# A hybrid attention and recurrence layer on one core: fewer and larger slot transfers, evictions on two engines, attention work written later

## The chip, the cores and the metric

The kernel runs on one core of a Trainium2 chip. The core has a matrix engine (TensorE, PE in the profile; its weight loads stand apart as PEld), a vector engine (VectorE, DVE), a scalar engine (ScalarE, ACT), a general engine (GpSimd, POOL) and an engine that here only issues transfers (SyncE, SP). Each takes its own instructions in the order in which they were written into its stream, and waits on semaphores for the others. Transfers between main memory and the on-chip memory run on 16 DMA engines; nearly all are issued by SP, one after the other.

The metric is the device time of one execution, in microseconds (us). A profile is one execution; it gives the time of every instruction, and the clock that was granted to TensorE.

## The reference

One layer, for 256 prompt tokens (context) and 1024 latent tokens: a normalisation, one large input projection, and two groups of heads side by side, whose outputs go through one output projection.

```
h = rmsnorm(x, norm_g) * (1 + scale) + shift
u = h @ w_in
q, k, v, g_a, u_b, g_b = split(u)
o_a = diff_attention(q, k_all, v_all, lam, ...) * silu(g_a)      # 8 heads, two score maps each
o_b, s_final = rwkv_branch(u_b, g_b, s0, lp)                     # 16 heads of 64
x = x + gate * (concat([o_a, o_b]) @ w_out)
y = rmsnorm(x, final_g)
```

Attention subtracts one softmax from another before it multiplies the values. The recurrent branch runs once forward and once backward over the tokens, with a 64 x 64 state per head:

```
def diff_attention: p = softmax(q @ k / 8);  a = p[0] - lam * p[1];  o = a @ v
def step(S, inp):
    sa = einsum('bhvk,bhk->bhv', S, -kk_t)
    S = S * w_t + sa[..., None] * b_t + v_t[..., None] * k_t
    return S, einsum('bhvk,bhk->bhv', S, r_t)
```

Beside the two outputs the layer returns the new keys and values of the prompt and the final states.

## The kernel before

**First stage.** The input projection, in blocks of 128 columns, with the shifts, decays and rotations that follow from each block. What the recurrence needs later goes to main memory: `kt` (keys, corrections and the small triangular matrices of a chunk), `ra` (queries), `vb` (values), and a triangular inverse (`td`) that GpSimd works out (`inverse`).

**Second stage** (`mix_phase`). The recurrence runs over chunks of 32 tokens. Two chunks make a part, eight chunks (a segment of 256 tokens) an item; there are 10 items, 40 parts and 80 chunks, called ticks here. Four pairs of heads run at a time, as two duos (`w` = 0 and 1), each with both directions. Each duo has two slots, used in turn by even and odd parts. A slot is a tile `L` (the matrices of a part) and a tile `R` (its right-hand sides: state, values, corrections).

- `load_part` (L766) loads a part into its slot, one part ahead: after a slot's last reader, the output products of the part before the last. `load_inv` (L787) loads the inverses into a tile `Tb`, one per duo, from three buffers (`TBUF`).
- `prep` (L794) multiplies the inverses into the slot: 32 small products into the bank `yb` (L802) and four copies by ScalarE into `L` (L805). It is written ahead of the second tick of the part before.
- `step` is one tick: correction products (L894), four copies of them per duo into `R` by ScalarE (L899); state products (L908), a multiplication by the decays into the next state by VectorE (L917); output products (L931) and one copy per duo into `ys` (L933). `store_y` writes four ticks of outputs.
- `fill` is called at two places of a tick. It lets attention run on by as many pieces as a credit allows (`RATE`, 0.86 of an even spread), and moves the inverse, the normalisations (`norm`) and the output projections (`project`) on by a piece.

Attention takes 80 blocks (8 heads, 10 blocks of 128 queries). A block over latent tokens has three chunks of keys per score map: scores (L1047), scaling with running minimum by VectorE (L1050), exponential by ScalarE (L1058); then the weight of the second map (L1070 to L1072), the combination of the two maps (`combine`, L1078), transposes (`trans`, L1086, copied by ScalarE at L1088) and the products with the values (L1101). Before the change the combination, transposes and values of a block are written among the scores of the block after it.

`norm` turns the recurrence's outputs into gated ones, `output` does so for attention, with `NDEL` and `ODEL` pauses. `project(j)` multiplies two heads of each group by their rows of `w_out` (L1286 to L1288) and adds to a sum in main memory (`acc`: loaded at L1268, added at L1280, stored at L1282); the last one, `final`, adds the residual and normalises. Projections 0 and 1 are started when the first five items are done, 2 and 3 after the last item.

The order on each engine is made by a scheduler that simulates the program; the order of the text is the priority, and `ahead(500)` raises the priority of what stands under it.

## Time and profile before

| | |
|---|---|
| median of 3 runs | 2642.7 us (2634.27 to 2647.06) |
| the profiled execution | 2639.98 us, of which 2637.7 us from the first to the last instruction (the span) |
| first stage, and the way into the second | 0 to 1243 us |
| recurrence (80 ticks) with attention, normalisations, projections 0 and 1 | 1243 to 2395 us |
| rest: last attention blocks, projections 2 and 3, final normalisation | 2395 to 2638 us |
| busy over the span: PE, DVE, ACT, POOL | 90%, 56%, 48%, 45% |
| mean clock granted to TensorE | 0.939 |

Times in profile rows are in us from the start of the span, unless marked ns. In a row of waits stand the waiting engine, tile and line, what ended the wait, then the total, the number and the longest. In a row of a group stand line, engine, operation, tiles (out<-in), shapes and count, then busy time and mean ns of one, then the engine's idle time ahead of them and what ended it.

### The profile page before, as it was taken

The page shows a single profiled execution, that of the slowest core. Times are in us where ns is not written, and L with a number is a line of the kernel's source. Part 1 is how long each engine was busy: PE and PEld are TensorE (multiplying, and loading weights), DVE is VectorE, ACT ScalarE, POOL GpSimd, SP SyncE. Part 2 cuts the span into 40 slices and gives each one's busy share as a digit, 9 for nine tenths or more (in the row PEclk, how much of TensorE's full clock was granted, in tenths as well). Part 3 has the DMA queues.
Part 4 walks back from the last instruction along what each step waited for, and adds up shares of the span by engine and source line. Part 5 has one row for each costly group of instructions (what it writes and reads, how often), then busy time and mean ns, then how long its engine had stood idle before and what let it go on. Part 6 is the DMA issues. An engine that isn't in the chain of part 4 may idle for free. (4 is left out here: it accounts for less than half of the span.)

```text
span 2637.7 us, 61554 instructions
## 1 busy us (share of the span) xinstructions
PE 2361.2 (90%) x23907; PEld 1908.8 (72%) x23907; DVE 1475.6 (56%) x2960; ACT 1274.8 (48%) x2928; POOL 1199.6 (45%) x1735
## 2 busy tenths in 40 slices
PE   6999999999999999998688888888889898898886
PEld 4788888888888888786466766666666676676664
DVE  5656565555455655434457556664455455566466
ACT  3334443333333433322476666766556357674243
POOL 4234344243433443375365525747467542125386
PEclk9999999999999999998798889889989999999997
DMA  7465656565645565567878777878867887676534
GB/s 237 111 165 131 177 147 176 135 169 161 160 129 155 136 176 131 167 158 185 176 155 187 162 160 145 184 164 191 211 155 194 203 198 171 141 171 220 176 104 161
DMA packets 532418, 437.63 MB, mean 166 GB/s; under 512 B 161991, under 2 KB 466291, under 8 KB 532128
## 3 DMA queue, kind: packets, MB, share of 16 engines
q1 hardware_dynamic: 530032, 427.96, 64.9%
q0 software_dynamic: 2096, 5.75, 1.1%
q8 instruction: 188, 3.08, 0.5%
q14 instruction: 102, 0.84, 0.1%
HBM read 258.69 MB, written 163.86 MB: 160 GB/s over the span
## 5 line engine op out<-in xcount | busy, mean ns | idle before, releaser
L1047 PE MATMUL sc<-ka,q 128*128 128x512 f32 (+1 forms) x832 | 296.7, 457 | 20.2 <-DVE pb L1050 12.3
L1050 DVE TENSOR_SCALAR_CACHE_REDUCE pb<-sc,mn 128x512 f32<-128x512 f32 x256 | 191.7, 749 | 135.1 <-PE sc L1047 110.4
L1101 PE MATMUL po<-vk,aT 128*128 128x128 f32 x1600 | 244.8, 296 | 9.1 <-ACT aT L1088 8.6
L1058 ACT ACTIVATE pb<-pb,mn 128x1536 f32<-128x1536 f32 (+1 forms) x160 | 218.4, 1366 | 60.2 <-DVE pb L1050 58.7
L1101 PEld LDWEIGHTS po<-vk,aT 128*128 128x128 f32 x1600 | 221.3, 205 | 29.4 <-ACT aT L1088 12.2
L479 POOL TENSOR_SCALAR ta<-ta,ka 128x256 f32<-128x256 f32 x80 | 88.1, 1101 | 297.8 <-DVE bk L477 297.7
L734 POOL TENSOR_TENSOR tmp<-aw,tt 128x31 f32<-128x31 f32 (+15 forms) x310 | 164.6, 531 | 127.9 <-DMA aw<-kt 54.9
L456 ACT COPY km<-ptk 64x256 f32<-64x256 f32 x320 | 117.4, 367 | 192.1 <-PE ptk L453 165.7
L899 ACT COPY R<-bank 32x128 f32<-32x128 f32 x640 | 163.4, 255 | 68.7 <-PE bank L894 59.4
L917 DVE TENSOR_TENSOR R<-bank,wc 64x256 f32<-64x256 f32 x312 | 131.4, 421 | 113.5 <-PE bank L908 98.4
L736 POOL TENSOR_TENSOR tt<-tt,tmp 128x31 f32<-128x31 f32 (+15 forms) x310 | 182.4, 588 | 18.2
L1047 PEld LDWEIGHTS sc<-ka,q 128*128 128x128 f32 x832 | 145.6, 208 | 55.7 <-DVE pb L1050 21.5
L1078 DVE SCALAR_TENSOR_TENSOR pb<-pb,cc,pb 128x512 f32<-128x512 f32 (+1 forms) x208 | 170.6, 866 | 2.5
L805 ACT COPY L<-yb 32x384 f32<-32x384 f32 x312 | 146.3, 469 | 40.1 <-PE yb L802 35.9
L802 PE MATMUL yb<-L,Tb 32*32 32x96 f32 x2496 | 96.1, 261 | 76.3 <-DMA L<-kt 68.7
L450 DVE TENSOR_TENSOR km<-pg,msk 128x512 f32<-128x512 f32 x80 | 55.1, 689 | 183.5 <-PE pg L449 168.7
L1050 DVE TENSOR_SCALAR_CACHE_REDUCE pb<-sc 128x512 f32<-128x512 f32 (+1 forms) x160 | 101.2, 635 | 91.2 <-PE sc L1047 75.3
L1088 ACT COPY aT<-pa 128x512 f32<-128x512 f32 (+1 forms) x208 | 115.9, 570 | 62.9 <-PE pa L1086 60.5
L1086 PE MATMUL pa<-ident,pb 128*128 128x128 f32 x800 | 133.2, 292 | 14.0 <-ACT acc L1278 7.8
L802 PEld LDWEIGHTS yb<-L,Tb 32*32 32x32 f32 x2496 | 62.6, 111 | 105.9 <-DMA L<-kt 56.3
L908 PEld LDWEIGHTS bank<-R,L 128*64 128x64 f32 x2560 | 99.3, 151 | 54.6 <-ACT R L899 23.7
L908 PE MATMUL bank<-R,L 128*64 128x64 f32 x2560 | 122.9, 243 | 16.7 <-ACT R L899 16.4
(355 smaller groups left out, 6463.2 us busy)
## 6 DMA issues: line engine op xcount, KB each, us to landing
kt<-km SPq DMA_DIRECT2D x160, 256.0 KB
L<-kt SPq DMA_DIRECT2D x80, 512.0 KB
acc<-acc SPq DMA_DIRECT2D x50, 512.0 KB
ra<-ra SPq DMA_DIRECT2D x160, 128.0 KB
L<-ra SPq DMA_DIRECT2D x160, 128.0 KB
R<-vb SPq DMA_DIRECT2D x320, 32.0 KB
y<-ys SPq DMA_DIRECT2D x160, 64.0 KB
yn<-y SPq DMA_DIRECT2D x20, 512.0 KB
```

The lines of the kernel that those rows point to most:

```text
L734: e.tensor_tensor(mv, aw[:n, t, t + 1:CH].unsqueeze(2).broadcast_to([n, w, j]), tt[:n, t:t + 1, 0:j].broadcast_to([n, w, j]), op=ALU.mult)
L736: e.tensor_tensor(tt[:n, t + 1:CH, 0:j], tt[:n, t + 1:CH, 0:j], mv, op=ALU.add)
L802: nc.tensor.matmul(pp[32 * q:32 * q + 32, n:n + 96], Tb[96:128, e, HN * q + c, :], L[96:128, e, q // 2, q % 2, c, 0:96], start=True, stop= ...
L805: nc.scalar.copy(L[96:128, :, q // 2, q % 2, :, 0:96], pp[32 * q:32 * q + 32, 0:192 * HN].rearrange("p (e c y) -> p e c y", e=2, y=96))
L899: nc.scalar.copy(R[96:128, k, e, :, hv(h)], bank[w][u:u + 32, 0:128].rearrange("p (d v) -> p d v", d=2))
L908: nc.tensor.matmul(bank[w][hv(h), o_:o_ + 64], L[:, e, h, d, k, 0:64], R[:, k, e, d, hv(h)], start=True, stop=True, tile_position=(0, 64 * h))
L1047: nc.tensor.matmul(sc, q[:, v, m, qc], ka[:, m, 0:kn], start=(v == 0), stop=(v == 1))
L1050: nc.vector.tensor_scalar(pm[:, c * 512:c * 512 + kn], sc, -0.125, mn[:, c - 1:c] if c else None, op0=ALU.mult, op1=ALU.min, accum_out=mn[ ...
L1058: nc.scalar.activation(v, v, AF.Exp, bias=mn[:, c:c + 1], scale=-1.0, accum_out=B["l3"][:, m, k:k + 1])
L1078: nc.vector.scalar_tensor_tensor(a, B["p"][1][:, v], B["cc"], a, op0=ALU.mult, op1=ALU.add)
L1086: nc.tensor.transpose(pt[:, t * P:(t + 1) * P], B["p"][0][:, 512 * c + t * P:512 * c + (t + 1) * P], ident)
L1101: nc.tensor.matmul(po, B["aT"][c][:, t * P:(t + 1) * P], vk[:, t, :], start=(c == 0 and t == 0), stop=(c == last and t == nt - 1))
```

## The change

- The scratch tensors `ra`, `kt` and `y` are laid out by duo (for `y` by four pairs), so that a duo's `kt` and `ra` are each one transfer, and a duo's values of two chunks one per direction (`R` is turned to [chunk, direction, pair] for it). A part takes 2 transfers of `kt`, 4 of `vb`, 2 of `ra`, and 1 of the inverses for both duos: 9 where there were 16. Outputs are stored in 4 transfers per four ticks instead of 8. `norm` reads its input in 2 transfers instead of 1.
- `Tb` is one tile for both duos, in one buffer instead of three tiles of half the size.
- The first duo's `prep` is written behind the correction copies of a part's second tick, the second duo's behind the tick's output products. Both stood ahead of that tick.
- The correction copies of the second duo go to VectorE. Only evictions are raised in priority now, the products are not. The output products stand beside the state products: the second `fill` comes after both.
- Attention: weight and combination are written at the end of the block itself, transposes among the next block's second scores, the values behind them or in the block after that; the sum of the exponentials goes straight to its place without a copy, and there is a third buffer for the transposed weights.
- Pace: 1.06 of an even spread in the first half of the ticks and 0.68 in the second, instead of 0.86 throughout; longer pauses in `norm`, `output` and the projections; projections 2 and 3 are started after the seventh item instead of the last.
- In `final` the residual is added by VectorE instead of GpSimd.

```diff
-RATE = 0.86
-TBUF = 3
-NDEL = 6
-ODEL = 8
+RATES = (1.06, 0.68)
+TBUF = 1
+NDEL = 10
+ODEL = 14
...
-    scratch("ra", [H, 5, NF, HD, 2, 2, HN * HD])
-    scratch("kt", [H, 5, NF, HD, 2, 2, HN * P])
+    scratch("ra", [H // 2, 5, NF, HD, 2, 2, 2, HN * HD])
+    scratch("kt", [H // 2, 5, NF, HD, 2, 2, 2, HN * P])
...
     def load_part(j):
...
-            nc.sync.dma_start(L[64:128].rearrange("r e h d c y -> r e (h d c y)"),
-                              s["kt"][p:p + 2, sg + 1, f].rearrange("e r h d y -> r e (h d y)"))
-            for e in range(2):
-                nc.sync.dma_start(L[0:64, e, :, :, :, 64:128].rearrange("r h d c y -> r (h d c) y"),
-                                  s["ra"][p + e, sg + 1, f].rearrange("r h d (c y) -> r (h d c) y", y=HD))
+            nc.sync.dma_start(L[64:128].rearrange("r e h d c y -> r (e h d c y)"),
+                              s["kt"][p // 2, sg + 1, f].rearrange("r e h d y -> r (e h d y)"))
+        load_inv(j)
+        for w in duos:
...
             for d in range(2):
                 t0 = tok0(sg, d) + CH * HN * (NF - 1 - f if d else f)
-                for c in range(HN):
-                    t1 = t0 + CH * (HN - 1 - c if d else c)
-                    nc.sync.dma_start(R[64:96, c, :, d, :], s["vb"][t1:t1 + CH, p * P:(p + 2) * P].rearrange("t (e v) -> t e v", e=2))
+                src = s["vb"][t0:t0 + CH * HN, p * P:(p + 2) * P].rearrange("(c t) y -> t c y", t=CH)
+                nc.sync.dma_start(R[64:96, :, d].rearrange("t c e v -> t c (e v)"), src[:, ::-1] if d else src)
+            nc.sync.dma_start(L[0:64, :, :, :, :, 64:128].rearrange("r e h d c y -> r (e h d c) y"),
+                              s["ra"][p // 2, sg + 1, f].rearrange("r e h d (c y) -> r (e h d c) y", y=HD))
...
     def load_inv(j):
-        for w in duos:
-            Tb = cp.tile([P, 2, 4 * HN, CH], F32, tag="Tb", name=f"Tb{w}_{j}", bufs=TBUF)
...
+        Tb = cp.tile([P, NL, 4 * HN, CH], F32, tag="Tb", name=f"Tb{j}", bufs=TBUF)
...
     def step(j, k, fill):
-        with ahead(HPC):
-            for w in duos:
...
-                        nc.scalar.copy(R[96:128, k, e, :, hv(h)], bank[w][u:u + 32, 0:128].rearrange("p (d v) -> p d v", d=2))
-        fill(0)
         with ahead(HPC):
             for w in duos:
...
+                        (nc.vector.tensor_copy if w else nc.scalar.copy)(
+                            R[96:128, k, :, e, hv(h)], bank[w][u:u + 32, 0:128].rearrange("p (d v) -> p d v", d=2))
+        later_prep = k == HN - 1 and j + 1 < n_part
+        if later_prep:
+            prep(j + 1, 0, yb)
+        fill(0)
...
-        fill(1)
...
+        for w in duos:
+            nc.scalar.copy(ysb[m, g][:, c % 4, 2 * w:2 * w + 2], bank[w][:, P:2 * P].rearrange("p (e v) -> p e v", e=2))
+        if later_prep:
+            prep(j + 1, 1, yb)
+        fill(1)
...
-        q.dma_start(y.rearrange("p t d v -> p t (d v)"), s["y"][p // 2, cols].rearrange("(t p) d v -> p t (d v)", p=P))
+        for t in range(2):
+            q.dma_start(y[:, t].rearrange("p d (h v) -> p (d h) v", h=2),
+                        s["y"][p // NL, g0 * P + t * P:g0 * P + (t + 1) * P, :, :, p % NL // 2].rearrange("p d h v -> p (d h) v"))
...
-            if p is not None:
-                weight(p)
-                combine(p, 0)
-            if pp is not None:
-                values(pp, len(st[pp]["ch"]) - 1)
+                if c < nk - 1 and vp:
+                    old_values()
+                    yield 0.87
+            while vp:
+                old_values()
                 yield 0.87
...
+            for c in range(max(nk, kp_)):
+                if c < kp_:
+                    trans(p, c)
+                    yield 0.43
+                if c < nk:
+                    scores(n, 1, c)
+                    yield cost
+            if new:
+                weight(n)
+                for c in range(nk):
+                    combine(n, c)
+            if kp_ > 1:
+                values(p, 0)
+                yield 0.87
...
-                nc.gpsimd.tensor_tensor(x, x, y, op=ALU.add)
+                nc.vector.tensor_tensor(x, x, y, op=ALU.add)
...
-            state["credit"] += rate / 2
+            state["credit"] += total / (4 * n_tick) * RATES[2 * state["t"] // n_tick]
...
-        if k == HN - 1 and j + 1 < n_part:
-            for w in duos:
-                prep(j + 1, w, yb)
...
-        if sg == 3:
+        if sg == (3 if m < 5 else 0):
```

What this does to the order on the engines is shown at three places. In the rows the tiles `L_11593` and `L_11583` are the second duo's slots (odd and even parts), `L_11573` and `L_11563` the first duo's; `bank_12298` and `bank_12299` (before) and `bank_12282` and `bank_12283` (now) are the banks of the first and the second duo.

TensorE before, ahead of the second duo's `prep` for part 15: from the last reading of the second duo's odd slot by output products to the first `prep` products on the newly loaded slot.

```order
L931 MATMUL bank_12299<-R_11594,L_11593 32x64 x8
L931 MATMUL bank_12298<-R_11564,L_11563 32x64 x8
L1047 MATMUL sc_6_1_2_17587<-ka_2_15907,q_1_15910 128x512 x2
L1047 MATMUL sc_7_0_0_17700<-ka_0_14697,q_1_15910 128x512 x2
L1101 MATMUL po_5_17599<-vk_0_14700,aT_5_0_17555 128x128 x4
L1086 MATMUL pa_5_2_17604<-ident,pb_12302 128x128 x4
L1101 MATMUL po_5_17599<-vk_1_16177,aT_5_1_17597 128x128 x4
L1047 MATMUL sc_7_0_1_17704<-ka_1_15904,q_1_15910 128x512 x2
L894 MATMUL bank_12299<-R_11584,L_11583 32x64 x8
L802 MATMUL yb<-L_11593,Tb_15_17192 32x96 x16
```

TensorE now, two parts later (part 17): the last rows ahead of the same duo's `prep`, with its first. The last reading of the slot `L_11593` stands four rows further up.

```order
L893 MATMUL bank_12283<-R_11584,L_11583 32x64 x8
L1057 MATMUL sc_1_0_1_17455<-ka_1_17068,q_0_16494 128x512 x2
L1147 MATMUL pxo_7_0_17464<-ident,ob_4_16304 128x128 x2
L803 MATMUL yb<-L_11573,Tb_17399 32x96 x13
L1057 MATMUL sc_1_0_2_17459<-ka_2_17071,q_0_16494 128x512 x2
L803 MATMUL yb<-L_11573,Tb_17399 32x96 x3
L913 MATMUL bank_12283<-R_11584,L_11583 64x64 x8
L913 MATMUL bank_12282<-R_11564,L_11563 64x64 x8
L1057 MATMUL sc_1_1_0_17518<-ka_0_15974,q_0_16494 128x512 x2
L1057 MATMUL sc_1_1_1_17544<-ka_1_17068,q_0_16494 128x512 x2
L936 MATMUL bank_12283<-R_11584,L_11583 32x64 x8
L803 MATMUL yb<-L_11593,Tb_17399 32x96 x10
```

Before, the second duo's `prep` follows its slot's release within a few rows of attention and ahead of the tick's state products. Now a tick's corrections, state products and output products and the first duo's `prep` stand between; the first duo's `prep` still comes close behind the corrections.

SyncE before, in the fifth item: transfers of one odd part, with what stands among them.

```order
L775 DMA L_11573<-ra 64x8x64
L772 DMA L_11573<-kt 64x2x1024
L945 DMA y<-ys_1_17307 32x4x128 x4
L775 DMA L_11573<-ra 64x8x64
L781 DMA R_11574<-vb 32x2x128 x2
L962 DMA yn_2_18246<-y 128x2x512
L792 DMA Tb_18_18202<-td_16550 32x2x256
L1150 DMA oT<-ga_7_18114 128x512
L1030 DMA vk_3_18340<-va 128x2x128
L775 DMA L_11593<-ra 64x8x64
L772 DMA L_11593<-kt 64x2x1024
L945 DMA y<-ys_1_17307 32x4x128 x4
```

SyncE now, in the fifth item.

```order
L781 DMA R_11594<-vb 32x2x256
L772 DMA L_11593<-kt 64x2048
L781 DMA R_11594<-vb 32x2x256
L782 DMA L_11593<-ra 64x16x64
L781 DMA R_11574<-vb 32x2x256
L772 DMA L_11573<-kt 64x2048
L781 DMA R_11574<-vb 32x2x256
L953 DMA y<-ys_1_17499 32x4x256 x4
L782 DMA L_11573<-ra 64x16x64
L971 DMA yn_2_18486<-y 128x4x128
L971 DMA yn_2_18491<-y 128x4x128 x2
L793 DMA Tb_18431<-td_16703 32x4x256
```

Both duos' slots are loaded in half the rows and close to one another, and one store of the outputs stands among them instead of two; the inverses' load comes at the end, for both duos.

VectorE now, at the end of a head, where before there were no correction copies (they were ScalarE's, at L899).

```order
L924 TENSOR_TENSOR R_11564<-bank_12282,wc_12308 64x4x64 x2
L1074 RECIPROCAL cc_7_18512<-l_4_17937 128x1
L1075 SCALAR_TENSOR_TENSOR cc_7_18512<-cc_7_18512,l_4_17937,neglam 128x1
L1081 SCALAR_TENSOR_TENSOR pb_12286<-pb_12287,cc_7_18512,pb_12286 128x512 x3
L1060 TENSOR_SCALAR pb_12287,mn_8_18768<-sc_8_1_0_18798 128x256
L1060 TENSOR_SCALAR pb_12286,mn_9_18888<-sc_9_0_0_18890 128x256
L1074 RECIPROCAL cc_8_18769<-l_8_18766 128x1
L1075 SCALAR_TENSOR_TENSOR cc_8_18769<-cc_8_18769,l_8_18766,neglam 128x1
L1081 SCALAR_TENSOR_TENSOR pb_12285<-pb_12287,cc_8_18769,pb_12285 128x256
L901 COPY R_11584<-bank_12283 32x2x64 x4
```

The second duo's four correction copies (L901) stand behind reciprocals that wait for ScalarE's exponentials, and behind combinations.

More of the change, by code (lines that the diff above doesn't have):

```diff
@@ L106, in tile_kernel @@
     scratch("gate", [2, D])
-    scratch("y", [(heads + 1) // 2, T, 2, 2 * P])
+    scratch("y", [heads // NL, T, 2, 2, NL // 2, P])
     scratch("acc", [T, D])
@@ L809, in mix_phase @@
         load_part(j)
-        load_inv(j)
         yield
@@ L886, in step @@
         hv = lambda h: slice(64 * h, 64 * h + 64)
-        with ahead(HPC):
-            for w in duos:
-                L, R = slots[w, j % 2]
-                for d in range(2):
-                    for e in range(2):
-                        for h in range(2):
-                            u = 64 * e + 32 * h
-                            nc.tensor.matmul(bank[w][u:u + 32, 64 * d:64 * d + 64], L[0:96, e, h, d, k, 96:128],
-                                             R[0:96, k, e, d, hv(h)], start=True, stop=True, tile_position=(0, u))
+        for w in duos:
+            L, R = slots[w, j % 2]
+            for d in range(2):
                 for e in range(2):
@@ L898, in step @@
                         u = 64 * e + 32 * h
-                        nc.scalar.copy(R[96:128, k, e, :, hv(h)], bank[w][u:u + 32, 0:128].rearrange("p (d v) -> p d v", d=2))
-        fill(0)
+                        nc.tensor.matmul(bank[w][u:u + 32, 64 * d:64 * d + 64], L[0:96, e, h, d, k, 96:128],
+                                         R[0:96, k, d, e, hv(h)], start=True, stop=True, tile_position=(0, u))
         with ahead(HPC):
             for w in duos:
-                L, R = slots[w, j % 2]
+                R = slots[w, j % 2][1]
                 for e in range(2):
-                    for d in range(2):
-                        for h in range(2):
-                            o_ = 256 + 128 * e + 64 * d
-                            nc.tensor.matmul(bank[w][hv(h), o_:o_ + 64], L[:, e, h, d, k, 0:64],
-                                             R[:, k, e, d, hv(h)], start=True, stop=True, tile_position=(0, 64 * h))
+                    for h in range(2):
+                        u = 64 * e + 32 * h
+                        (nc.vector.tensor_copy if w else nc.scalar.copy)(
[4 more added lines that the diff above has]
+        fill(0)
+        for w in duos:
+            L, R = slots[w, j % 2]
+            for e in range(2):
+                for d in range(2):
+                    for h in range(2):
+                        o_ = 256 + 128 * d + 64 * e
+                        nc.tensor.matmul(bank[w][hv(h), o_:o_ + 64], L[:, e, h, d, k, 0:64],
+                                         R[:, k, d, e, hv(h)], start=True, stop=True, tile_position=(0, 64 * h))
+        with ahead(HPC):
+            for w in duos:
                 if k < HN - 1:
-                    dst = R[0:64, k + 1]
+                    dst = slots[w, j % 2][1][0:64, k + 1]
                 elif f == NF - 1 and sg == 3:
@@ L922, in step @@
             ysb[m, g] = cp.tile([P, 4, NL, HD], F32, tag="ys", name=f"ys{m}_{g}", bufs=YBUF)
-        with ahead(HPY):
-            for w in duos:
-                L, R = slots[w, j % 2]
-                for e in range(2):
-                    o_ = P + 64 * e
-                    for h in range(2):
-                        for d in range(2):
-                            q = 64 * d + 32 * h
-                            nc.tensor.matmul(bank[w][q:q + 32, o_:o_ + 64], L[:, e, h, d, k, 64:96], R[:, k, e, d, hv(h)],
-                                             start=True, stop=True, tile_position=(0, q))
-                nc.scalar.copy(ysb[m, g][:, c % 4, 2 * w:2 * w + 2], bank[w][:, P:2 * P].rearrange("p (e v) -> p e v", e=2))
+        for w in duos:
+            L, R = slots[w, j % 2]
+            for e in range(2):
+                o_ = P + 64 * e
+                for h in range(2):
+                    for d in range(2):
+                        q = 64 * d + 32 * h
+                        nc.tensor.matmul(bank[w][q:q + 32, o_:o_ + 64], L[:, e, h, d, k, 64:96], R[:, k, d, e, hv(h)],
+                                         start=True, stop=True, tile_position=(0, q))
+        for w in duos:
+            nc.scalar.copy(ysb[m, g][:, c % 4, 2 * w:2 * w + 2], bank[w][:, P:2 * P].rearrange("p (e v) -> p e v", e=2))
+        if later_prep:
+            prep(j + 1, 1, yb)
+        fill(1)
     def store_y(m, g):
@@ L1193, in attention, with old_values @@
             cost = 0.45 if nk == 3 else 0.25
+            vp = []
+            if pp is not None:
+                vp = [(pp, c) for c in range(1 if len(st[pp]["ch"]) > 1 else 0, len(st[pp]["ch"]))]
+            def old_values():
+                if vp:
+                    values(*vp.pop(0))
             for c in range(nk):
@@ L1220, in attention @@
                     load_q(h + 1, 2)
-            for c in range(kp_ - 1):
-                trans(p, c + 1)
-                yield 0.43
-                values(p, c)
-                yield 0.87
     TORD = (8, 9, 2, 3, 4, 5, 0, 1, 6, 7)
@@ L1386, in mix_phase @@
     total = heads * (8 * (6 * 0.45 + 3 * 1.3) + 2 * (4 * 0.25 + 1.3))
-    rate = total / (2 * n_tick) * RATE
     def at(t, f):
```

65 lines of the change are left out of this document (26 added, 39 removed).

## The prediction

> **What bounds the kernel now.** I read the page first, then the windows of the stages, the waits of the second stage, and the chain of waits.
>
> ```profile
> PE 2361.2 (90%) x23907; PEld 1908.8 (72%) x23907; DVE 1475.6 (56%) x2960; ACT 1274.8 (48%) x2928; POOL 1199.6 (45%) x1735
> ```
>
> ```profile
> 800.00:1000.00 200.00, 197.04 (x1494) 167.12 (x1493) 117.51 (x182) 80.14 (x156) 81.02 (x97) 0.99 0.59 155
> 1243.00:1700.00 457.00, 376.18 (x5563) 291.44 (x5566) 268.30 (x673) 300.48 (x779) 240.62 (x443) 0.87 0.81 170
> 1700.00:2395.00 695.00, 614.44 (x8140) 470.07 (x8139) 386.49 (x939) 431.31 (x1108) 322.58 (x561) 0.92 0.77 179
> 1243.00:2395.00 1152.00, 990.62 (x13695) 761.51 (x13694) 654.78 (x1612) 731.79 (x1886) 563.20 (x1004) 0.90 0.78 176
> 2395.00:2640.00 245.00, 189.29 (x900) 149.92 (x898) 146.91 (x296) 81.97 (x169) 136.34 (x149) 0.89 0.48 162
> ```
>
> The columns of a window are its length, the busy time of PE, PEld, DVE, ACT and POOL, the clock granted to TensorE, the DMA share and GB/s. TensorE is the bound: 99% busy at clock 0.99 in the first stage, which the change leaves alone. In the second stage, 1152 us long, it stands idle for 1152 - 991 = 161 us, and the clock is 0.90. Both idle time and clock can give something. DVE and ACT are busy 57% and 64% there.
>
> ```profile
> PE yb L802 <- DMA L<-kt: 68.7, 31, 10.1
> PE bank L908 <- ACT R L899: 16.4, 16, 3.3
> PE bank L894 <- ACT ys L933: 13.0, 10, 2.7
> PE sc L1047 <- DVE pb L1050: 9.1, 9, 4.1
> PE pso L1286 <- DVE acc L1280: 8.5, 2, 8.2
> PE pa L1086 <- ACT acc L1278: 7.8, 2, 5.9
> PE po L1101 <- ACT aT L1088: 7.8, 8, 3.1
> PE sc L1047 <- DMA ka<-klo: 7.4, 2, 6.3
> PE bank L931 <- DVE R L917: 4.5, 6, 2.1
> ```
>
> These are TensorE's waits in that stage (total, number, longest). One stands out: `prep` waits 68.7 us for slots. Behind a `prep` that waits, everything on TensorE waits. The chain of waits carries those transfers too:
>
> ```profile
> 1875.23 4.93 DMA R<-vb
> 1909.02 4.81 DMA L<-kt
> 2226.57 8.60 DMA L<-kt
> ```
>
> **a) Slots, -40 us.** A load starts when the slot's last output product is done, and lands some 5 us later (4.8 and 4.9 above; 8.6 when late). Covered is what TensorE streams between that product and the next `prep` on the slot. I counted that over both orders of instructions, with the pitch of each kind from rows like these:
>
> ```profile
> 1502.62 0.43 PE L931 MATMUL bank<-R,L 128*32 128x64 f32 x16
> ...
> 1504.33 0.71 PE L1047 MATMUL sc<-ka,q 128*128 128x512 f32 x2
> 1504.88 1.05 PE L1101 MATMUL po<-vk,aT 128*128 128x128 f32 x8
> ...
> 1509.07 0.85 PE L802 MATMUL yb<-L,Tb 32*32 32x96 f32 x28 [1.43 <-DMA L<-kt]
> ```
>
> One score product takes 0.28 to 0.30 us (the next piece starts 0.55 after a pair), one product of `po` 0.12, of L931 0.023, of `prep` 0.028. The median over 76 slots goes from 5.1 us to 7.4: for the first duo from 4.45 to 5.2, for the second from 5.95 to 9.7. By these pitches the stage streams 656 us, and takes 1152: one streamed us stands for 1.76 real ones. So the first duo gains 1.3 us, the second 6.6. Going through the waits of `prep` one by one (the row of 1509.07 is one, 1.43 us), 54 us in 24 fall to the first duo, 22 in 13 to the second; their mean is about 2. A cover of 6.6 more ends the second duo's 22; 1.3 more takes 24 x 1.3 = 31 at most, since the shorter waits end sooner: I take 18. That is -40, bounds 0 and -69. The shorter issue helps, but I add nothing for it:
>
> ```profile
> L772 SPq DMA_DIRECT2D L<-kt x80: 573/590/1082, 1203.5 to 2356.9; - x80
> L775 SPq DMA_DIRECT2D L<-ra x160: 512/597/1756, 1204.2 to 2359.1; - x160
> L781 SPq DMA_DIRECT2D R<-vb x320: 302/425/1629, 1205.9 to 2360.4; - x160
> L792 SPq DMA_DIRECT2D Tb<-td x80: 302/378/1876, 1223.8 to 2337.6; - x80
> L945 SPq DMA_DIRECT2D y<-ys x160: 302/441/1881, 1300.0 to 2398.5; - x160
> ```
>
> The three numbers are ns least, median and most. A part (of 40) takes 2 x 0.59 + 4 x 0.60 + 8 x 0.43 + 2 x 0.38 = 7.7 us of SP; now 9 issues, at these medians 4.6. The store that stood between goes from 8 issues (3.5 us) to 4.
>
> **b) Correction copies, -6 us.** Behind them wait the state products: 16.4 us (L908, above).
>
> ```profile
> L899 ACT COPY R<-bank 32x128 f32<-32x128 f32 x640 | 163.4, 255 | 68.7 <-PE bank L894 59.4 <-PE bank L931 1.0
> L917 DVE TENSOR_TENSOR R<-bank,wc 64x256 f32<-64x256 f32 x312 | 131.4, 421 | 113.5 <-PE bank L908 98.4 <-DMA wc<-wc 5.6 <-ACT aT L1088 3.6
> ```
>
> Eight copies in a row on ScalarE take 8 x 0.255 = 2.0 us a tick, two engines with four each 1.0. That is some 1 us off a wait of 1.0 in the mean, but in 16 waits only; I take a third, -6, bounds 0 and -16, and upward the rival below. VectorE's copy is not in the trace; its nearest row, L917, takes 421 ns for twice the rows and twice the columns. I take 0.2 (bounds 0.1 and 0.42): 320 x 0.2 = 64 us on an engine that idles for 1152 - 655 = 497.
>
> **c) Attention's waits, -6 us.** `po` on `aT` and `sc` on `pb` wait 16.9 us, `pa` 7.8 on an eviction of the projection. With values written a chunk later and a third buffer for `aT` the 7.8 of `po` can go. I take -6, bounds 0 and -21.
>
> **d) Clock, -22 us.** From the first stage (busy 99%, clock 0.99) to 1700 to 2395 (88%, 0.92) and 1243 to 1700 (82%, 0.87) the clock falls by 0.7 to 0.8 points for a point of busy time. a) to c) take away 52 us, 4.5 points: clock 0.90 becomes 0.936, and 991 us of busy time become 953. Since busy rows hold fixed parts too, I take a little over half of these 38; bounds 0 and -45.
>
> **e) Rest, -14 us.**
>
> ```profile
> L1286 PE MATMUL pso<-wohi,ohi x80: 387/390/796, 2400.2 to 2505.0; 128*128 128x512 f32 x80
> 2400.00:2420.00 20.00, 12.52 (x48) 9.33 (x48) 1.37 (x2) 0.00 (x0) 0.96 1.01 345
> 2411.15 6.32 DMA acc<-acc
> L1358 POOL TENSOR_TENSOR x<-x,y 128x1024 f32<-128x1024 f32 x10 | 24.9, 2487 | 3.3 <-DMA x<-x_sample 2.6 <-DMA x<-x_prompt 0.7
> L1364 DVE SCALAR_TENSOR_TENSOR y<-x,fss,fgb 128x1024 f32<-128x1024 f32 x10 | 12.9, 1294 | 0.8
> ```
>
> After the stage projection 2 runs in ten blocks of 24 products, 105 us in all, its `acc` transfers on the chain. In the new order two of them stand ahead of the last output products: -21 in the rest, and +2 x 24 x 0.26 = +12 in the stage (48 products took 12.5 us). The residual's addition takes 2.49 us on GpSimd; VectorE takes 1.29 for a pass of the same size. Ten blocks would give -12, but most are covered by the last projection's products: -5. Sum -14, bounds 0 and -25.
>
> **f) One buffer for `Tb`, +5 us.** The load now waits for the last `prep` of the part before.
>
> ```profile
>   DMA Tb<-td: 7.7, 2
> ```
>
> With three buffers `prep` hardly waited for it (this row: 7.7 us in two). Between the last `prep` of a part and the first of the next I count 12 streamed us in the median (before, from the buffer's release, 23), 5.7 in the lowest tenth, 4.2 at least: 21, 10 and 7.4 real, against a landing of 5 and an issue behind up to nine others. Only the shortest can be late: +5. Were the cover gone, 38 parts at 2.2 us (68.7 / 31) would be +84.
>
> **g) `norm`'s input in two transfers, 0.**
>
> ```profile
> L970 POOL TENSOR_TENSOR yn<-yn 128x512 f32<-128x512 f32 x16 | 21.0, 1310 | 54.7 <-DMA yn<-y 46.4 <-issue 4.3 <-DMA R<-vb 1.8
> ```
>
> GpSimd waits 46 us for it and still stands at 49%; four more pauses ahead of its result cover it. Without that cover one more issue per tile, 20 x 0.5 = +10, is the upper bound.
>
> Sum: -40 - 6 - 6 - 22 - 14 + 5 = -83. The profiled execution took 2640.0 (span 2637.7), 2.7 us below the median of 2642.7, which I neglect: **2557 us**.
>
> **Rivals.** *Forecast*: 2557, within 30: **0.40**.
>
> *The clock stays.* Without d): **2579**, chance **0.08**. [...]
>
> *The loads are the bound.* DMA share is 0.81 in the stage's first part, as many bytes move as before, and loads that start earlier in number of products may land no earlier. Then a) and d) give nothing: 2640 - 21 = **2619**. Against it: landings of 5 us where waits are 2. Chance **0.15**.
>
> *The second duo's corrections queue on VectorE* (the other side). ScalarE had them to itself; VectorE waits there:
>
> ```profile
> DVE l L1070 <- ACT pb L1058: 77.7, 44, 6.0
> L1078 DVE SCALAR_TENSOR_TENSOR pb<-pb,cc,pb 128x512 f32<-128x512 f32 (+1 forms) x185 | 149.0, 851 | 2.1
> ```
>
> The weight waits 1.8 us in the mean for exponentials, and three combinations of 0.85 follow, now in one go: up to 1.8 + 2.6 us ahead of four copies that state products of all heads wait for. Between corrections and state products TensorE has about 2.7 streamed us, 4.8 real, of other work; the rival decides where the copies end later than that. At 1.8 us in each of 80 ticks it costs +144 and eats d): 2640 - 40 - 6 - 14 + 5 + 144 - 29 (the slot waits that a) leaves, hidden by longer ticks) = **2700**. Against it: the wait for exponentials is shorter than the cover, and only some ticks meet a head's end. Chance **0.12**.
>
> *All waits go.* With a), c), d), e) at their lower bounds and b) at -16: 2640 - 69 - 16 - 21 - 45 - 25 = **2464**; I put the case at 2464 to 2510, chance **0.17**. For it: SP's shorter queue, which I left at nothing.
>
> *`Tb` takes the place of the wait removed.* 2557 + 84 - 5 = **2636**, chance **0.08**; it decides if the load is issued over 5 us after its release.
>
> **How the numbers follow.** About 0.5%, 13 us, is what a measurement of this kernel can tell from no change. Faster: 0.40 + 0.08 + 0.15 + 0.17 = 0.80. Same: `Tb`, 0.08. Slower: 0.12. The range leaves out the queue on VectorE and the lower half of "all waits go", 0.20: 2485 to 2640. The forecast's own range is 2527 to 2587.
>
> **What would show it.** In the new profile: a) `prep` waits below 30 us on `L`, the second duo's gone; b) L913 waiting below 10 us on `R`, VectorE's L901 near 0.2 us; if L913 waits tens of us on VectorE, the other side holds. d) Clock 0.93 or more over the second stage. e) 64 products of `pso` per row after the last output product instead of 80. f) `prep` on `Tb` below 10 us. g) No TensorE wait behind `yn`. If `prep` waits as before with DMA share above 0.8, the loads were the bound. By the sum the stage ends at 2395 - 40 - 6 - 6 - 22 + 5 + 12 = 2338; the forecast is wrong if its last output product comes over 30 us later.

## The result, and the profile after

| | before | after |
|---|---|---|
| median of 8 runs | 2637.1 us (2633.7 to 2647.1) | 2610.8 us (2598.7 to 2623.7) |
| profiled execution, span | 2640.0, 2637.7 us | 2612.4, 2610.6 us |
| ratio, 95% interval | | 0.9895 [0.9868, 0.9922] |
| last output product of the recurrence | 2395 us | 2383 us |
| first product of the last projection | 2506 us | 2506 us |
| TensorE idle and busy, 1243 us to that last output product | 161 and 991 us | 137 and 1003 us |

The kernel became 1.05% faster, 26 us, where 83 were forecast. (Other orders of the same two programs, further down, put the gain nearer 0.7%.) The first table of the page shows TensorE's busy time nearly unchanged (2361.2 before):

```profile
PE 2363.7 (91%) x23907; PEld 1902.6 (73%) x23907; DVE 1559.8 (60%) x3210; ACT 1192.9 (46%) x2606; POOL 1166.5 (45%) x1725
```

The windows of the kernel after, for the second stage and the rest (columns as in the prediction: length, PE, PEld, DVE, ACT, POOL, clock, DMA share, GB/s):

```profile
1243.00:2383.00 1140.00, 1003.22 (x13736) 766.13 (x13736) 734.02 (x1857) 651.81 (x1564) 550.28 (x993) 0.90 0.82 178
2383.00:2611.00 228.00, 179.45 (x860) 138.74 (x856) 151.09 (x303) 80.39 (x169) 121.49 (x149) 0.92 0.51 170
```

The clock of the stage stands at 0.90, where it stood. The stage is 12 us shorter and the rest, 243 us before, 15. TensorE's waits in the second stage after, in the form of the prediction's list:

```profile
PE yb L803 <- DMA L<-kt: 59.5, 23, 10.4
PE yb L803 <- DMA Tb<-td: 15.2, 4, 8.3
PE pa L1089 <- DVE acc L1292: 7.1, 3, 5.3
...
PE bank L936 <- DVE R L924: 6.8, 11, 2.9
PE sc L1057 <- DVE pb L1060: 6.3, 11, 1.5
PE bank L893 <- ACT ys L939: 6.1, 4, 2.4
...
PE bank L913 <- ACT R L901: 4.3, 8, 1.0
```

Most of the small waits fell: the state products' for `R` from 16.4 to 7.9 (4.3 for ScalarE's copies, 3.6 for VectorE's), the corrections' from 13.0 to 6.1; that of the values on `aT` (7.8) is gone from the list. The large one did not: `prep` waits 74.7 us for slots and inverses, 68.7 before. The group of its products says the same, with 76.3 us of idle time ahead of them before:

```profile
L803 PE MATMUL yb<-L,Tb 32*32 32x96 f32 x2496 | 105.3, 269 | 81.1 <-DMA L<-kt 59.5 <-DMA Tb<-td 15.2 <-DMA y<-ys 3.4
```

Going through those waits one by one by duo: the second duo's fell from 22 us to 6, most of what was forecast. The first duo's rose from 54 us in 24 waits to 75 us in 26. This stretch of TensorE's timeline after shows one of them:

```profile
1511.30 0.65 PE L936 MATMUL bank<-R,L 128*32 128x64 f32 x32
1511.88 2.05 PE L1104 MATMUL po<-vk,aT 128*128 128x128 f32 x16
1513.77 0.38 PE L1089 MATMUL pa<-ident,pb 128*128 128x128 f32 x2
1513.91 0.71 PE L1057 MATMUL sc<-ka,q 128*128 128x512 f32 x2
1514.56 0.65 PE L893 MATMUL bank<-R,L 96*32 96x64 f32 x32
1515.14 0.44 PE L1089 MATMUL pa<-ident,pb 128*128 128x128 f32 x2
1515.42 0.61 PE L1104 MATMUL po<-vk,aT 128*128 128x128 f32 x4
1519.12 0.54 PE L803 MATMUL yb<-L,Tb 32*32 32x96 f32 x6 [3.09 <-DMA L<-kt]
```

The output products (L936) release both duos' slots at 1511.9. SP issues the loads 0.7 us later:

```profile
1512.64 1.11 SPq L772 DMA_DIRECT2D L<-kt  x2
```

They land at 1519.1, 7.2 us after the release and 6.5 after the issue; TensorE has 4 us of other work in between, and waits 3.09. The first duo's `prep` stands close behind the corrections (L893), the second duo's comes at 1528.7.

### The profile page after: what moved, and what is told of

Read it like the earlier page. It is cut to its first block, busy times and chain, and to the rows that moved or that the text cites. A ratio compares the mean times of both kernels' runs of the same rounds, so it can differ in the third digit from the quotient of the medians.

```text
span 2610.6 us, 60873 instructions
## 1 busy us (share of the span) xinstructions
PE 2363.7 (91%) x23907; PEld 1902.6 (73%) x23907; DVE 1559.8 (60%) x3210; ACT 1192.9 (46%) x2606; POOL 1166.5 (45%) x1725
## 4 chain that ended last, share of the span: by engine, by line
PE 55%; DMA 19%; DVE 8%; POOL 6%; SPq 5%; issue 3%; ACT 2%; POOLq 0%; DVEq 0%; ACTq 0%
DMA L<-kt 5%; PE sc L1057 5%; PE po L1104 4%; PE bank L913 3%; PE pa L1089 3%; PE yb L803 3%; PE pg L449 3%; DMA acc<-acc 2%; PE pso L1298 2%; DMA wst<-w_out 2%; PE pso L1299 1%; DMA Tb<-td 1%; PE pso L1300 1%; PE bank L936 1%; PE psg_v L335 1%
## 5 line engine op out<-in xcount | busy, mean ns | idle before, releaser
L1057 PE MATMUL sc<-ka,q 128*128 128x512 f32 (+1 forms) x832 | 302.3, 452 | 17.5 <-DVE pb L1060 9.3
L1104 PE MATMUL po<-vk,aT 128*128 128x128 f32 x1600 | 237.2, 289 | 0.9 <-ACT aT L1091 0.7
L479 POOL TENSOR_SCALAR ta<-ta,ka 128x256 f32<-128x256 f32 x80 | 81.1, 1014 | 292.8 <-DVE bk L477 292.7
L803 PE MATMUL yb<-L,Tb 32*32 32x96 f32 x2496 | 105.3, 269 | 81.1 <-DMA L<-kt 59.5
L1057 PEld LDWEIGHTS sc<-ka,q 128*128 128x128 f32 x832 | 137.8, 201 | 53.6 <-DVE pb L1060 20.1
L1089 PEld LDWEIGHTS pa<-ident,pb 128*128 128x128 f32 x800 | 97.2, 150 | 45.1 <-DVE acc L1292 13.1
```

The costliest lines, as they stand in the source:

```text
L803: nc.tensor.matmul(pp[32 * q:32 * q + 32, n:n + 96], Tb[96:128, e, HN * q + c, :], L[96:128, e, q // 2, q % 2, c, 0:96], start=True, stop= ...
L1057: nc.tensor.matmul(sc, q[:, v, m, qc], ka[:, m, 0:kn], start=(v == 0), stop=(v == 1))
L1089: nc.tensor.transpose(pt[:, t * P:(t + 1) * P], B["p"][0][:, 512 * c + t * P:512 * c + (t + 1) * P], ident)
L1104: nc.tensor.matmul(po, B["aT"][c][:, t * P:(t + 1) * P], vk[:, t, :], start=(c == 0 and t == 0), stop=(c == last and t == nt - 1))
```

## The experiments

Ratios are to the kernel before, each with its 95% interval; the changed kernel's is 0.9895. x1 to x4, x5 to x8, x9 to x12 and x13 to x16 each ran together on one chip, beside the kernel before; x17 ran later, on another chip. The kernel before took 2634 to 2640 us in these groups, so runs of different groups are best compared by their ratios.

**Where the first duo's `prep` stands.** Theory A: the slot waits come from `prep`'s place in TensorE's order. Theory B: the loads are the bound, whatever the order. The first two runs hold the first duo's `prep` on TensorE behind a product of the tick; they change no wait and no transfer. The run x1:

```diff
-                        nc.tensor.matmul(bank[w][u:u + 32, 64 * d:64 * d + 64], L[0:96, e, h, d, k, 96:128],
+                        last = nc.tensor.matmul(bank[w][u:u + 32, 64 * d:64 * d + 64], L[0:96, e, h, d, k, 96:128],
...
         if later_prep:
-            prep(j + 1, 0, yb)
+            with tc.issue_after(last.ins):
+                prep(j + 1, 0, yb)
```

> The changed kernel with one edge more: the first duo's prep products are held, on TensorE alone, behind the last correction product of the part's second tick; nothing is left out. In the changed kernel the first duo waits 75 us for its slots (24 waits), although its prep is written there: the planner places it where its own simulation has the load landed, some 6 streamed us after the slot's last reader. Theory A (the place in the order is too early for the real landing of 6 us and more): the streamed work between release and prep goes from 6 to 16 us in the median, the waits of prep on L and Tb fall from 75 to under 20 us in the second stage, and the time falls by 30 to 70 us. Theory B (the loads are the bound, DMA share 0.82): the waits come back as later ones, on prep or on the corrections behind it, and the time stays within 10 us.

In x2 `last` is the tick's last output product, and both `prep` stand behind the output products.

> As the run before, but the first duo's prep is held behind the tick's last output product, and the second duo's comes after it; nothing is left out. Theory A: slot waits near 0, but 64 products and eight copies of 0.47 us by ScalarE now stand between the last output products and the next corrections: these wait 2 to 4 us for the copies in each of 38 parts, so that the time gains less than in the run before or loses up to 60 us. Theory B: as the run before, within 10 us of the changed kernel.

x1 took **2561.7 us, 0.9724 [0.9690, 0.9758]**: 49 us less than the changed kernel, 45 by the ratios. Its waits and its second stage:

```profile
PE sc L1058 <- DVE pb L1061: 18.7, 24, 4.5
PE bank L937 <- DVE R L925: 13.5, 12, 4.0
...
PE yb L803 <- DMA Tb<-td: 9.5, 2, 8.8
...
PE yb L803 <- DMA L<-kt: 7.5, 1, 7.5
```

```profile
1243.00:2331.00 1088.00, 971.76 (x13695) 749.52 (x13690) 738.18 (x1855) 653.47 (x1561) 559.08 (x992) 0.91 0.85 186
```

Of 59.5 us on `L` one wait of 7.5 is left, while the DMA share rose from 0.82 to 0.85. The same bytes in less time, and hardly a wait for them: the loads were not the bound, and theory B falls. The stage ends at 2331 us, where the forecast had 2338. But idle time in the stage fell by 21 us only, since other waits grew (those for VectorE are the first two rows), and busy time by 31.

x2 took 2594.5 us, 0.9843 [0.9810, 0.9877]. Its slot waits fell to 9 us, but other waits grew (to 2383 us; its stage ends at 2415):

```profile
PE bank L934 <- DVE R L922: 22.0, 16, 6.6
PE bank L893 <- ACT ys L937: 15.6, 5, 6.3
PE sc L1057 <- DVE pb L1060: 14.0, 14, 3.8
PE pa L1089 <- DVE pb L1081: 12.8, 11, 10.1
```

By the ratios, a hold that is later than it need be gives two thirds of x1's further gain back. The wait that was expected to do it, corrections behind the copies of `prep`, isn't among these rows; the output products' wait for VectorE's decays is.

**The hold in the kernel before (x5).** Both duos' `prep` behind the last correction product; 16 small transfers, three buffers, all copies on ScalarE and the old attention stay.

```diff
-        if k == HN - 1 and j + 1 < n_part:
-            for w in duos:
-                prep(j + 1, w, yb)
         step(j, k, fill)
...
+        if k == HN - 1 and j + 1 < n_part:
+            with tc.issue_after(last.ins):
+                for w in duos:
+                    prep(j + 1, w, yb)
         fill(0)
```

> The kernel before with one edit: both duos' prep products are held, on TensorE alone, behind the last correction product of the part's second tick; its 16 smaller transfers, three buffers for the inverses, copies and attention stay. Theory A says that the place of prep in the order set the slot waits in the kernel before too (76 us there) and that the transfers' number has no part in it: the streamed work between release and prep goes from 6 and 8 us to 17 and 18, the waits on L fall under 20 us, and the time falls by 40 to 60 us, to about 2585. If the fewer and larger transfers were needed for it, waits of over 30 us stay and the gain is below 25 us.

2599.2 us, 0.9877 [0.9832, 0.9921]: this one edit gives as much as the whole change. Slot waits:

```profile
PE bank L894 <- ACT ys L937: 32.3, 14, 7.9
PE sc L1051 <- DVE pb L1054: 21.4, 13, 5.9
PE bank L912 <- ACT R L899: 21.2, 21, 4.5
...
PE yb L802 <- DMA L<-kt: 10.5, 2, 10.1
```

They fall to 10.5 us without any larger transfer, so theory A's account of the slot waits holds here too. Other waits took their place: the corrections wait for ScalarE (32.3, 13.0 before), as do the state products and, behind VectorE, the scores. Over the whole execution TensorE's idle time fell from 276.5 to 268.9 us only (the span less the busy time of the page); the rest of the gain of 35 us is busy time (2361.2 to 2334.7).

**The single buffer (x3).** One tile and one transfer per duo, `TBUF = 3`; `aT` back to two buffers to make room.

> The changed kernel with the inverses as before: one tile and one transfer per duo, three buffers; to make room for it the transposed weights go back to two buffers. Theory A with the single buffer as part of the loss: the waits of prep on Tb (15 us in 4, and one of 8 us at the start) go, and the time falls by 10 to 20 us, unless the waits on L take them over. Theory B: the time stays, waits on L grow by what those on Tb lose. Two buffers for the transposed weights may add up to 8 us (the values' waits before the change).

2608.2 us, 0.9892 [0.9858, 0.9926]: no change.

```profile
PE yb L804 <- DMA L<-kt: 71.7, 25, 9.7
...
PE yb L804 <- DMA Tb<-td: 3.9, 1, 3.9
```

The 15.2 us on `Tb` became 3.9, the 59.5 on `L` became 71.7: 74.7 and 75.6 together, and no time was gained. That the wait for `Tb` only took the place of one for `L` fits this, but the idle time ahead of `prep` also moves by as much between orders of the changed kernel (81.1 us, 67.6 in x9 and 75.6 in x10 below).

**The residual's addition (x4).** `nc.vector` back to `nc.gpsimd` in `final`.

> The changed kernel with the residual's addition in the final normalisation back on GpSimd; nothing else. From the start of the last projection to the end the profile takes 131 us before and 105 after, 27 less, as much as the whole gain. If the addition makes that gain, the time goes up by 15 to 27 us. If it was worth the 5 us that were forecast, and the rest of the 27 is attention work that is now done earlier, it goes up by 0 to 10 us.

2621.5 us, 0.9944 [0.9908, 0.9981], some 11 to 13 us slower than the changed kernel, between the two expectations. The second stage ends at 2383 us as in the changed kernel, so the loss lies in the rest: from the last projection on the profile takes 119 us instead of 105, and the addition 2.44 us on GpSimd against 1.69 on VectorE:

```profile
L1372 POOL TENSOR_TENSOR x<-x,y 128x1024 f32<-128x1024 f32 x10 | 24.4, 2436 | 8.0 <-DMA x<-x_sample 6.0 <-DMA x<-x_prompt 1.8
```

```profile
L1372 DVE TENSOR_TENSOR x<-x,y 128x1024 f32<-128x1024 f32 x10 | 16.9, 1690 | 9.8 <-POOL y L1371 9.8
```

The first row is x4's, the second the changed kernel's.

**How far an order scatters (x9, x10, x12).** The planner (the scheduler that makes the order) writes another order for any edit. x9 and x10 are the changed kernel at a pace of 1.05 and 0.69, and 1.07 and 0.67; x12 is the kernel before at 0.87.

> The changed kernel with a pace of 1.05 and 0.69 instead of 1.06 and 0.68: as good as the same program, but the planner writes another order. It measures how far the order alone scatters, on which the reading of the copies' run (44 us below the changed kernel with one edit) rests. If the order scatters little, 2600 to 2622 us; if runs of this kind differ by 20 us and more, the 44 us and the gain of the change itself are partly the luck of an order, and single edits below that size can't be priced by it.

> As the run before, with 1.07 and 0.67. Little scatter: 2600 to 2622 us. Great scatter: over 20 us away from the changed kernel or from the run before. In both the first duo's waits for slots should stay at 50 to 80 us, since the prep's place in the planner's order is still about 6 streamed us behind the release.

> The kernel before with a pace of 0.87 instead of 0.86: the same control for it. Little scatter: 2625 to 2645 us. Great scatter: over 20 us away from it.

2605.6 (0.9895), 2615.5 (0.9930) and, for the kernel before, 2618.6 us (0.9950 [0.9927, 0.9973]). The changed kernel's three orders lie within 10 us, the two of before 16 apart. An edit that moves the time by less than some 15 us is not priced by one run. The change itself is not far above that: its three orders have a mean ratio of 0.9907, the two of the kernel before 0.9975, a gain of 0.7% or 18 us. Nor does the time follow the slot waits from order to order: the kernel before has 76.3 us of idle time ahead of `prep`, x12 90.1, and x12 is the faster one.

**The split of the copies (x6, x8, x11, x13, x14, x16).** In x6 all correction copies go back to ScalarE; in x8 the same beside x1's hold; in x11 the second duo's go to VectorE in the kernel before.

```diff
-                        (nc.vector.tensor_copy if w else nc.scalar.copy)(
+                        nc.scalar.copy(
```

> The changed kernel with the second duo's correction copies back on ScalarE; nothing else. The forecast priced the split at 6 us: the state products' wait for R (7.9 us after, 16.4 before) goes back to about 16, and the time goes up by 5 to 15 us. If the slot waits hide it, as theory A has it for every wait of the first duo's neighbours, the waits of prep shrink by as much as those of the state products grow, and the time stays within 5 us.

> The run with the first duo's prep held behind the corrections (2561.7 us), and the second duo's correction copies back on ScalarE. There TensorE's largest waits are for VectorE (scores 18.7 us in 24, output products 13.5 in 12). If those come from the copies that VectorE took over, they fall by half and the time falls by 5 to 20 us; if the split is worth what the forecast gave it, the state products wait 8 us more and the time goes up by 5 to 15.

> The kernel before with the second duo's correction copies on VectorE, nothing else. The forecast: 6 us less, since the state products' wait of 16 us for R goes down by a third. If the split itself costs the 44 us that its undoing gave, the time goes up by 20 us or more, to 2655 to 2690, with VectorE's copies late behind its waits for exponentials (the weight's 78 us in 44) and state products waiting for them.

x6 took 2567.4 us, 0.9768 [0.9720, 0.9816]: 44 less than with the split, where 5 to 15 more were expected. x8 took 2554.8, 0.9693 [0.9638, 0.9749], 7 less than x1; x11 2638.6, 1.0012 [0.9989, 1.0034], no difference. (By the ratios, x6's 44 us are 33.) These three sizes did not agree, so x6 and x8 and x1 were run in other orders: x13 and x14 are x6 at the paces of x9 and x10, x15 is x1 and x16 x8 at that of x9.

> The changed kernel with all correction copies on ScalarE (2567 us, 44 under the changed kernel) and a pace of 1.05 and 0.69. If the copies' split costs what that run said, this one lies 30 to 55 us under its neighbour with the split at the same pace (2605.6): 2550 to 2575. If most of the 44 was one order's luck, it lies at 2585 to 2610.

> As the run before, with a pace of 1.07 and 0.67, where the kernel with the split takes 2615.5 us. If the split costs some 40: 2560 to 2585. If the 44 was luck: 2595 to 2620.

> The first duo's prep held behind the corrections (2561.7 us) with a pace of 1.05 and 0.69. Theory A (the slot waits were the place of prep, and an order's luck has little part in the 49 us): 2545 to 2580, 25 us and more under the neighbour without the hold (2605.6), slot waits below 25 us. If the order's luck made it: above 2585.

> The hold and all copies on ScalarE (2554.8 us) with a pace of 1.05 and 0.69. If split and slot waits are one matter (the wait that the split removes comes back at the slots, and where they don't wait it is worth nothing), it lies within 15 us of the run before; if the split costs 40 by itself, it lies 25 to 50 under it.

| | pace 1.06, 0.68 | 1.05, 0.69 | 1.07, 0.67 |
|---|---|---|---|
| changed kernel (split) | 0.9895 | 0.9895 | 0.9930 |
| all copies on ScalarE | 0.9768 | 0.9825 | 0.9777 |
| hold | 0.9724 | 0.9726 | |
| hold, all copies on ScalarE | 0.9693 | 0.9671 | |

x13 took 2589.6 us, x14 2580.7 and x15 2567.9. The hold stands: 1.7% in both orders with the split, 0.8 and 1.5% without it. The split costs 0.7 to 1.5% without the hold, 1.2% or 31 us in the mean, and 0.3 to 0.6% with it. So little of x6's gain was one order's luck. x16 is the fastest kernel of this study: **2551.8 us, 0.9671 [0.9642, 0.9700]**.

What the split costs is not seen in the waits: in x6 the state products wait 10 us longer for `R`, as forecast.

```profile
PE yb L803 <- DMA L<-kt: 45.5, 21, 5.5
PE bank L913 <- ACT R L901: 18.5, 15, 4.8
```

It stands in TensorE's busy time, for the same 23907 products. The first row is x6's, the second x13's, the third x14's; the changed kernel has 2363.7, x9 2368.6, x10 2369.9:

```profile
PE 2346.1 (91%) x23907; PEld 1892.2 (73%) x23907; DVE 1463.1 (57%) x2890; ACT 1274.7 (49%) x2926; POOL 1173.7 (46%) x1725
```

```profile
PE 2341.9 (90%) x23907; PEld 1887.4 (73%) x23907; DVE 1460.1 (56%) x2890; ACT 1276.0 (49%) x2926; POOL 1175.7 (45%) x1725
```

```profile
PE 2336.5 (91%) x23907; PEld 1889.7 (73%) x23907; DVE 1468.3 (57%) x2890; ACT 1274.8 (49%) x2926; POOL 1180.0 (46%) x1725
```

In the mean that is 26 us, while idle time (span less busy time) differs by 14 less, 15 more and 1 more in the three pairs.

**Where the hold's gain lies.** The same reading of the five pairs with and without the hold:

| | idle ahead of `prep`, us | TensorE idle, whole span | TensorE busy |
|---|---|---|---|
| changed kernel, x1 | 81, 25 | 247, 232 | 2364, 2325 |
| x9, x15 | 68, 18 | 233, 230 | 2369, 2340 |
| x6, x8 | 65, 25 | 233, 238 | 2346, 2323 |
| x13, x16 | 94, 25 | 248, 238 | 2342, 2310 |
| kernel before, x5 | 76, 13 | 277, 269 | 2361, 2335 |

The hold takes 40 to 69 us away ahead of `prep`, but all idle time together changes by 15 less to 5 more: other waits come in the place of the slot waits. Most of the gain is that the same products keep TensorE busy for 23 to 39 us less. A part of it stands at `prep` itself, whose row was 105.3 us in the changed kernel. In x1:

```profile
L803 PE MATMUL yb<-L,Tb 32*32 32x96 f32 x2496 | 85.3, 264 | 25.1 <-DMA Tb<-td 9.5 <-ACT L L806 7.7 <-DMA L<-kt 7.5
```

Two things in the traces go with shorter busy time, for the hold as for the split. The clock records hold stretches at full and at half clock only (53 of each in the trace of the kernel before, 46 in that of the changed kernel), and from 1243 us on the busy time at half clock falls with the hold in all five pairs (203 to 168 us in the first) and is 23 us less in the mean without the split. And the products come in fewer runs, a run being neighbours of one line: 2564 in the changed kernel, 2462 in x1; 2615 in the mean with the split, 2538 without. Over all 19 profiles the busy time from 1243 us on, with the part at half clock counted half, goes with the number of runs (correlation 0.93, 0.15 us a run). That is an association; no run changed one of the two alone, and the cause of the shorter busy time stays open.

**The pace (x7) and the early projections (x17).** x7: `RATES = (0.86, 0.86)`. x17: `if sg == 3` again, for projections 2 and 3.

> The changed kernel with attention's pace at 0.86 of an even spread throughout, as before, instead of 1.06 and 0.68. The forecast gave the pace no term. If it matters, attention work moves from the first half of the ticks into the second, the busy share of 1243 to 1700 falls from 86% toward the 82% of before, and the time goes up by 10 us or more; if it does not, the time stays within 8 us.

> The changed kernel with projections 2 and 3 started after the last item, as before; nothing else. In its order 216 products of the projection stand behind the last output product, 192 in the changed kernel, 240 before. The forecast had two blocks moved as worth 9 us net (21 in the rest against 12 in the stage). By it, the time goes up by about 5 us, within what orders scatter; if the early start is worth nothing, or costs, since other work moves back in its place, the time stays or falls by 5 to 20 us.

2602.9 us, 0.9897 [0.9845, 0.9949], and 2595.8 us, 0.9853 [0.9812, 0.9895]. The pace makes no difference. Without the early start the kernel is not slower, rather 10 to 15 us faster, which is at the edge of what orders scatter; there is no sign of the 9 us that the forecast gave it.

## Why the prediction was wrong

**a) Slots: the step that failed.** Forecast -40, measured +5 (76.3 to 81.1 us of idle time ahead of `prep`). The second duo's part was mostly right: -22 forecast, -16 measured. The first duo's was "1.3 us more cover, 18 us less", and came out at +21. The step had three faults. First, the count took each product of the order as one of the trace; but the recurrence's and the values' products stand in the trace twice (1280 products of L936 in the order, 2560 in the profile). With that mended the first duo's cover is 5.9 us before and 6.1 after, its lowest quarter 4.9 both times, and the second duo's 7.7 and 12.4: nothing was to be had for the first duo. (The orders shown with the change are both of part 15; the second is not "two parts later".)

Second, the landing was put at 5 us, from two pieces of the chain. Where the first duo's `prep` waited, it began 7.7 us after the slot's release before (median of 24 waits) and 7.4 us after (of 26); TensorE had other work for 5.4 and 5.5 us of that. So its usual wait stayed, 1.8 and 1.7 us. The 21 us more are a few long waits: those over 4 us were two of 16 us together, and are six of 44 us now. What held these loads up, no run shows.

Third, a slot wait was priced as time lost in full. The table above has the holds remove 40 to 69 us of them, and TensorE's idle time hardly falls.

What the change's text said of `prep` was a trap too. The new place in the text, behind the corrections, is not what sets its place in the order: that lies some 6 streamed us (products times their pitch, without waits) behind the slot's release in both kernels. Written elsewhere in the text (both ahead of the tick, or behind its output products) it comes to stand 5.8 and 6.6 us behind it by the order. That the planner puts it where its own simulation has the load landed is argued from these orders. That the place makes the slot waits is shown: held 16.5 streamed us behind (x1), 52 of 59.5 us are gone. That the transfers' size is not needed for this is shown by x5: it keeps the small ones, and its waits on `L` are down to 10.5 us; the joined ones alone left 59.5.

**b) Copies.** -6 forecast. The wait it was worked from fell as it should (16.4 to 7.9), VectorE's copy took 0.29 us, between the bounds of 0.1 and 0.42. But the split as a whole costs some 31 us in this kernel without the hold, which no row of a wait shows, and nothing in the kernel before (x11). The rival of a queue on VectorE priced a loss of 144 by state products that wait for VectorE; they wait 3.6 us. The sign was that of the rival, the mechanism was not.

**c) Attention.** -6 forecast, -21 its bound. All waits counted, `po` went by -8, the scores by -3, `pa` by +2 and the projection's products by -10 (14.8 to 4.5): more than forecast, within the bound.

**d) Clock.** -22 forecast, by the 52 us of waits that should go. Idle time in the stage fell by 24 us (161 to 137); by the slope of the prediction that gives a clock of 0.91 to 0.92, and it stayed at 0.90. So the slope failed too. The changed kernel and x16 are both busy for 88% of the stage, at 0.90 and 0.92, and x7 for 89%, at 0.89. x16's row, then x7's:

```profile
1243.00:2320.00 1077.00, 951.74 (x13650) 738.27 (x13652) 634.45 (x1530) 725.74 (x1873) 553.82 (x984) 0.92 0.85 186
```

```profile
1243.00:2360.00 1117.00, 991.71 (x13704) 768.33 (x13704) 732.55 (x1842) 650.87 (x1556) 550.21 (x980) 0.89 0.82 181
```

Long waits do not account for the clock either: the trace of the kernel before has 37 stretches at half clock in the stage, 232 us together, and only six TensorE waits over 4 us. What sets it stays open.

**e) Rest.** Busy time in the stage rose by the 12 us forecast for the two blocks (991 to 1003, the sum of all rows), but the rest didn't get their 21 back: the last projection starts at 2506 us as before, with 64 products of each of the three lines behind the stage instead of 80, by the order. The eight blocks left take longer, with other work between them; x17 shows no gain from the early start. The residual's addition was mis-sized: 11 to 13 us instead of 5 (x4). That it hid less behind the last projection than assumed is argued: GpSimd had 94 us of work in the last 132 of the kernel before.

```profile
2506.00:2638.00 132.00, 95.93 (x468) 77.25 (x466) 89.22 (x168) 52.52 (x119) 94.04 (x89) 0.87 0.38 132
```

Forecast -26 in the rest and +12 in the stage; measured -15 and +12.

**f) and g).** `prep` waits 15.2 us for `Tb` where 5 were forecast, and x3 finds no time lost by it. TensorE has no wait behind `yn`.

**The rivals.** "The loads are the bound" gave 2619, nearest to the 2611 measured, and said what would be seen: waits as before at a DMA share above 0.8. Both were seen, and it is wrong all the same: at 0.85 x1 hardly waits. "The clock stays" had the clock right, and by itself would have given 2579. "`Tb` takes the place" was half right: 15 us of waits for it, of which x3 finds no loss. The forecast of 2557 is close to what x1 takes (2562), but that is luck in the parts: against the kernel before, x1 has 51 us less idle time ahead of `prep` where a) and f) had 35, 6 us more of other idle time in the stage where b) and c) had 12 less, and 18 us less in the rest where e) had 26.

## What to carry to other kernels

Whether a buffer's load was waited for was settled here by the work that stands between the buffer's release and its next use, in the order that the engine gets: with 16.5 streamed us there instead of some 6, 52 of 59.5 us of waits went (x1). Count that work for each consumer apart, in the trace's own units, and compare it with the time from release to landing (7.2 us in the stretch shown); a median over two groups hides the one that binds (here 5.9 and 6.1 us before and after for the first duo, 7.7 and 12.4 for the second). Where a planner sets the order, the place of a step in the text is no evidence of its place on the engine; hold it there if it matters. Do not price a wait by its row: after an edit compare all idle time and the busy time of the same work, since one wait can make room for another (the holds took 40 to 69 us away ahead of `prep`, and all idle time changed by 15 less to 5 more). And measure how far the time moves for an edit that means nothing (10 us in three orders of one kernel here, 16 in two of the other) before a single edit is priced.

## What was not expected

- The DMA share rose from 0.82 to 0.85 as the waits for DMA vanished (x1): a high share beside waits did not mean that transfers bound the kernel.
- With the slot waits gone, TensorE's idle time was nearly what it had been; the time went down because TensorE was busy for less (five pairs).
- The same 23907 products keep TensorE busy for 2310 us in x16 and 2364 in the changed kernel, at a clock of 0.92 and 0.90 in the second stage.
- One part of the change (the split of the copies) made the kernel slower by some 31 us, while the wait behind these copies became shorter (16.4 to 7.9 us).
